# A decoder layer on one core: other buffers and another place for the first feed-forward weights and read-backs

## The chip, the core and the metric

The kernel runs on one core of a Trainium2 chip. A core has a matrix engine (TensorE, here PE, with its weight loads as PEld), three engines for element work (VectorE or DVE, ScalarE or ACT, GpSimd or POOL) and a queue engine (SyncE or SP) that here only issues transfers. Each works off its own queue in order; semaphores order them against each other. The metric is the device time of one execution in microseconds (us).

## What is computed

One layer of a decoder on 1024 tokens of width 1024, all in float32: a projection, four heads of a gated delta rule, four heads of differential attention, an output product with a residual, and a gated feed-forward part of width 2816. The change touches the end of attention, the output product and the feed-forward part:

```python
proj = rms_norm(h, norm1_w[l]) @ w_in[l]
...
mix = jnp.concatenate([o_a.reshape(B_, S_, DN_V), o_b.reshape(B_, S_, DF_V)], axis=-1)
h = h + mix @ w_out[l]
u = causal_dwconv(rms_norm(h, norm2_w[l]) @ w_up[l], ffn_conv_w[l], ffn_conv_b[l])
gate, up = jnp.split(u, 2, axis=-1)
h = h + (jax.nn.silu(gate) * up) @ w_down[l]
```

## The kernel before

**Products in three.** Each float32 matrix is split into a high part (a copy by ACT into a shorter form) and a low part (what is left, a subtraction by DVE or POOL); a product is then three matmuls, high by high, high by low and low by high. `split_w` (line 200) does it for weights, `mm3` (line 382) issues the three matmuls.

**Buffers.** Tiles are 128 partitions by 1024 columns and come from pools with a fixed number of buffers each: "g" has 16, "w" 5, "raw" 3 (loads from memory), "l" 2, "j" 2, "c" 4. A tile that wants a buffer waits until an earlier tile of the same pool has seen its last reader. A planner puts the instructions of each engine in an order ahead of time: by their place in the program, moved forward by the number that `part(name)` takes from the table `PRI` (line 36), and by when it thinks their inputs and buffers are there.

**From attention to the feed-forward part.** Attention runs head by head over eight row tiles of 128 tokens; in the last head the tiles run from 7 down to 0. `wout_a` (line 1030) multiplies the first half of the mixed heads with the output weights during heads 1 to 3 and keeps the result in memory. `wout_b` (line 1107) does the second half in the last head, one row tile at a time: load, product, residual, normalization, transposes (`norm_T`), and `combine` (line 1069). Its eight weight tiles (two column halves `c`, two row halves, high and low) take their buffers from the list `spare` in line 1111, and POOL makes their low parts (line 204).

**The up product by seven products.** The normalized activations are cut in token halves and width halves, the weights in gate and up and in width halves, and these two-by-two products are done with seven block products rather than eight. `combine` stores the blocks "11" and "21" for tiles 7 to 4, and for tiles 3 to 0 the block "22", the combination T2 (in its two parts) and the rests T1, T3 and T4, which `mv_split` (line 1211) splits afterwards. `product` (line 1222) is 12 matmuls of 128x512. `up_early` (line 1246) does the products "11" and "21" of the first two of 22 weight tiles ahead of the others, since they need only tiles 7 to 4; its load is held back until a named result of the last head (`o3`) exists, by a one-element copy on POOL into the load's buffer (line 1249). `up` (line 1260) loads a weight tile, forms four sums on POOL, splits them, and issues T2, "11", T1, T3, "21", "22" and T4; the result goes through the depthwise convolution, `silu` and the gate and is written to `act_dram`, 128 rows for each `j`. It uses four "c" buffers (cg, cu and two acc).

**The down product.** `down` (line 1318) runs over the two column halves, and in each over 11 pairs of 128 rows of the activations: it loads and splits the pair's weights, reads the two activation tiles back from `act_dram` (line 1336), splits them (lines 1338 and 1339) and issues 48 matmuls into eight PSUM banks, one for each row tile. The banks are in two pools of four; `bank(i, s)` takes one from pool `i % 2`, and the last up tile (j = 21) uses pool 1.

Of the kernel before, what the change touches and what calls it, by code (L numbers as in the profile page):

```python
# [34 lines left out]

PRI = dict(dprep=1000, dscan=930, dinv=200, dout=100, dproj=100, dz1=100, qk0=370, v0=400,
           d_dec=0, d_k=-25, d_q=0, d_nat=50, d_sc=800, d_v=0, d_w=-430, qkn=970, qks=25, a2o=0,
           prep0=160, attn1=0, attn2=0, attn3=25, prep=-25, fill=0, wa=0, wb1=0, wb2=25, ffn=110)
FS = [2, 1, 2, 3, 2, 2, 2, 2]
PP0, PP1 = 4, 2  # L40
PRE_K = {5: 1, 6: 0}
# [17 lines left out]
def hybrid_layer(ctx, tc, x, positions, norm1_w, w_in, dn_conv_w, dn_a_log, dn_dt_bias,  # L59
# [1009 lines left out]
    def combine(pss, u, tt):  # L1069

        o = slice(tt % 4 * P, tt % 4 * P + P)
        by = lambda ap: ap.rearrange("p (k t) -> p k t", t=P)
        if tt == NT - 1:
            mv_new("11")
            mv_new("21")
        if tt == 3:
            mv_new("22")
            mv_new("T2")
        if tt >= 4:
            if tt % 2 == 1:  # L1080
                stage[tt], stage[tt - 1] = ([gt("k1"), gt("k4")],) * 2
            half = slice(tt % 2 * 512, tt % 2 * 512 + 512)
            for q, name in enumerate(("11", "21")):
                hv, lv = (t[:, :, o] for t in stage[name])
                S.activation(hv, by(pss[q]), AF.Copy)
                V.tensor_tensor(lv, by(pss[q]), hv.bitcast(F32), op=ALU.subtract)
                S.activation(stage[tt][q][:, half], pss[q], AF.Copy)
            return
        b12, b22 = pss
        t1, t4 = (t[:, tt % 2 * 512:tt % 2 * 512 + 512] for t in stage[tt + 4])  # L1090
        t2 = u[:, 0:512]
        if tt % 2 == 1:
            stage["T3"] = stage.get("T3", []) + [gt("t3")]
        t3 = stage["T3"][-1][:, tt % 2 * 512:tt % 2 * 512 + 512]
        S.activation(t3, b12, AF.Copy)
        V.tensor_tensor(t1, b12, t1, op=ALU.subtract)
        V.tensor_tensor(t2, b22, t1, op=ALU.subtract)
        V.tensor_tensor(t3, b22, t3, op=ALU.subtract)
        hv, lv = (t[:, :, o] for t in stage["22"])
        S.activation(hv, by(b22), AF.Copy)  # L1100
        V.tensor_tensor(lv, by(b22), hv.bitcast(F32), op=ALU.subtract)  # L1101
        hv, lv = (t[:, :, o] for t in stage["T2"])
        S.activation(hv, by(t2), AF.Copy)
        G.tensor_tensor(lv, by(t2), hv.bitcast(F32), op=ALU.subtract)
        G.tensor_tensor(t4, t4, t2, op=ALU.subtract)

    def wout_b():

        w2row = gt("w2row")
        nc.scalar.dma_start(w2row, norm2_w.broadcast_to([P, D]))  # L1110
        spare = itertools.chain([wt] * 5, [ltr] * 2, [jtr])
        wfs = [load_wo(4, c, G, lambda s: next(spare)(s)) for c in range(2)]

        def tile_(tt):
# [90 lines left out]
    def bank(i, s):  # L1205
        return pf[i % 2].tile([P, 512], F32, tag="b", name=nm(s))
# [1 line left out]

    act_dram = dp.tile([FFN, T], F32, name="act_dram")

    def mv_split(name, src, lo_eng):

        tiles = [[gtr("x" + name) for _ in range(2)] for _ in range(2)]
        mv[name] = [[tiles[p][k // 2][:, k % 2 * 512:k % 2 * 512 + 512] for k in range(4)] for p in range(2)]
        for tt in (3, 2, 1, 0):
            sv = src(tt).rearrange("p (k t) -> p k t", t=P)
            for i in range(2):
                hv, lv = (tiles[p][i].rearrange("p (k t) -> p k t", t=512)[:, :, tt * P:tt * P + P] for p in range(2))
                S.activation(hv, sv[:, 2 * i:2 * i + 2], AF.Copy)
                lo_eng.tensor_tensor(lv, sv[:, 2 * i:2 * i + 2], hv.bitcast(F32), op=ALU.subtract)  # L1220

    def product(ps, w, name, start):

# [14 lines left out]
    def raw_(s="raw"):  # L1238
        return rp.tile([P, T], F32, tag="raw", name=nm(s))
# [5 lines left out]

    def up_early(j):

        e_raw = raw_()
        G.tensor_copy(e_raw[:, 0:1], o3[1][:, 0:1])
        load_half(e_raw, 0, j * P, 8)  # L1250
        w11, w12 = halves(split_w(e_raw, None, T, gtr))
        kept = gt("early")
        e = bank(1, "pe")
        product(e, w11, "11", True)
        S.activation(kept[:, 0:512], e, AF.Copy)  # L1255
        product(e, w12, "21", False)
        S.activation(kept[:, 512:1024], e, AF.Copy)
        return kept
# [59 lines left out]
    def down():  # L1318
        pairs = [(i, i + 1) for i in range(0, NF, 2)]
        kept = None  # L1320
        for c in range(2):
            cs = slice(c * 512, (c + 1) * 512)
            pss = [bank(1 - tt // 4, "pd") for tt in range(NT)]
            order = pairs if c == 0 else pairs[::-1]
            for pr in order:
                raw = raw_()
# [5 lines left out]
                else:  # L1332
                    hl = []
                    for i in pr:
                        g_ = ct_("act")
                        nc.sync.dma_start(g_, act_dram[i * P:(i + 1) * P, :])
                        gh, gl = gtr("gh"), gtr("gl")
                        S.activation(gh, g_, AF.Copy)  # L1338
# [22 lines left out]
                    V.tensor_tensor(rv[:, i, :], pss[tt], rv[:, i, :], op=ALU.add)  # L1361
                    nc.sync.dma_start(out2[tt * P:(tt + 1) * P, cs], rv[:, i, :])

    with part("ffn"):
        early = [up_early(j) for j in range(EARLY)]
    mv_split("T1", lambda tt: stage[tt + 4][0][:, tt % 2 * 512:tt % 2 * 512 + 512], V)
    mv_split("T3", lambda tt: stage["T3"][1 - tt // 2][:, tt % 2 * 512:tt % 2 * 512 + 512], V)
    mv_split("T4", lambda tt: stage[tt + 4][1][:, tt % 2 * 512:tt % 2 * 512 + 512], G)
    for j in range(NF):
        up(j, early[j] if j < EARLY else None)  # L1370
    down()
# [28 lines left out]
```

## Time and profile before

| | us |
|---|---|
| median of 3 runs | 1448.12 |
| lowest and highest | 1446.78 and 1448.77 |
| the profiled execution, its own time | 1446.19 |
| its span, first to last instruction | 1444.5 |
| PE busy | 1340.6 |
| DVE busy | 886.0 |
| ACT busy | 612.0 |
| POOL busy | 388.2 |

Busy time is the sum of the instructions' durations on an engine; a matmul's end is modelled, so a full PE is not PE at its peak. The granted clock is PE's, as a share of full speed. In a timeline, the brackets behind an instruction give the idle time of its engine before it and what ended that; where an engine waited for several things, it is the one that came last.

### The profile page before, as it was taken

Reading aid. Unit: us, or ns where it says so; the run is one execution under the profiler, and the core shown is the slowest. Engines: PE = TensorE matmul, PEld = TensorE weight load, DVE = VectorE, ACT = ScalarE, POOL = GpSimd, SP = SyncE. Lnnn points to the kernel's source line nnn. Section 1 sums busy time; section 2 is a strip of 40 time slices with the busy share of each in tenths; the row PEclk is TensorE's granted clock in tenths of the full one; section 3 lists DMA queues with packets and bytes.
Section 4 is the critical chain, followed back from the end, with each engine's and each line's share of the span. In section 5 each row is a group of like instructions: output and inputs, shape, how many; then the busy total and the mean of one; then the engine's idle time right before and its main releaser. Section 6 shows DMA issues by size and latency. Waiting matters only on the chain. (4 is left out here: it accounts for less than half of the span.)

```text
span 1444.5 us, 20625 instructions
## 1 busy us (share of the span) xinstructions
PE 1340.6 (93%) x7927; PEld 1128.8 (78%) x7927; DVE 886.0 (61%) x1745; ACT 612.0 (42%) x1098; POOL 388.2 (27%) x307
## 2 busy tenths in 40 slices
PE   7998898989979998998878999999999988999998
PEld 7877676888979986786656788888888876888887
DVE  5467978886343378886778666666666655324322
ACT  6445454532334456573545444343434434222220
POOL 3044313130341253321035434444433320000000
PEclk8999999999999999999998999999999998999999
DMA  7221112131743357443521222222222237447421
GB/s 222 84 79 36 39 30 74 43 91 59 194 107 94 117 154 187 113 126 102 175 81 44 88 82 79 88 88 78 82 88 85 76 120 276 144 160 215 150 88 59
DMA packets 143393, 155.14 MB, mean 107 GB/s; under 512 B 9279, under 2 KB 114367, under 8 KB 143295
## 3 DMA queue, kind: packets, MB, share of 16 engines
q1 hardware_dynamic: 130815, 144.14, 31.3%
q0 software_dynamic: 11008, 8.39, 3.1%
q10 hardware_dynamic: 1472, 1.29, 0.3%
q8 instruction: 62, 1.02, 0.3%
q14 instruction: 36, 0.29, 0.1%
HBM read 111.32 MB, written 38.29 MB: 104 GB/s over the span
## 5 line engine op out<-in xcount | busy, mean ns | idle before, releaser
L383 PE MATMUL pd<-whi,gh 128*128 128x512 f32 x352 | 138.3, 393 | 7.0 <-ACT gh L1338 7.0
L385 PE MATMUL pd<-whi,gl 128*128 128x512 f32 x352 | 138.1, 392 | 0.7 <-DVE gl L1339 0.7
L204 POOL TENSOR_TENSOR wlo<-raw,whi 128x1024 fp32r<-128x1024 f32 x34 | 83.6, 2468 | 203.9 <-PE gT L424 68.7
L384 PE MATMUL pd<-wlo,gh 128*128 128x512 f32 x352 | 138.1, 392 | 0.0
L1315 POOL TENSOR_TENSOR acc<-acc,acc 128x1024 f32<-128x1024 f32 x22 | 53.5, 2432 | 241.6 <-issue 196.6
L403 PE MATMUL pn<-whi,xn 128*128 128x256 f32 x448 | 114.8, 290 | 0.0
L404 PE MATMUL pn<-whi,xn 128*128 128x256 f32 x448 | 114.2, 289 | 0.0
L1338 ACT ACTIVATE gh<-act 128x1024 fp32r<-128x1024 f32 x42 | 44.4, 1060 | 134.6 <-PE pd L384 113.8
L1339 DVE TENSOR_TENSOR gl<-act,gh 128x1024 fp32r<-128x1024 f32 x42 | 51.8, 1237 | 67.8 <-ACT gh L1338 67.6
L403 PEld LDWEIGHTS pn<-whi,xn 128*128 128x128 f32 x448 | 85.9, 192 | 0.4
L404 PEld LDWEIGHTS pn<-whi,xn 128*128 128x128 f32 x448 | 85.9, 192 | 0.1
L383 PEld LDWEIGHTS pd<-whi,gh 128*128 128x128 f32 x352 | 66.8, 190 | 21.5 <-ACT gh L1338 7.5
L206 DVE TENSOR_TENSOR wlo<-rx,whi 128x1024 fp32r<-128x1024 f32 x22 | 29.5, 1339 | 87.5 <-ACT whi L202 87.5
L202 ACT ACTIVATE whi<-raw 128x1024 fp32r<-128x1024 f32 x58 | 61.0, 1052 | 50.8 <-issue 18.3
L1230 PE MATMUL pa<-xT,whi 128*128 128x512 f32 x176 | 71.2, 404 | 9.2 <-DVE x L1101 4.8
L424 PE MATMUL gT<-xn,wlo 128*128 128x512 f32 x192 | 78.7, 410 | 0.0
L385 PEld LDWEIGHTS pd<-whi,gl 128*128 128x128 f32 x352 | 66.7, 190 | 15.2 <-DVE gl L1339 1.4
L422 PE MATMUL gT<-xn,whi 128*128 128x512 f32 x192 | 78.2, 407 | 0.0
L206 DVE TENSOR_TENSOR wlo<-raw,whi 128x1024 fp32r<-128x1024 f32 x24 | 30.1, 1254 | 78.3 <-PE pd L384 57.9
L423 PE MATMUL gT<-xn,whi 128*128 128x512 f32 x192 | 77.7, 405 | 0.0
L384 PEld LDWEIGHTS pd<-wlo,gh 128*128 128x128 f32 x352 | 66.8, 190 | 14.0
L1230 PE MATMUL pe<-x,whi 128*128 128x512 f32 x176 | 70.6, 401 | 5.5 <-ACT early L1255 4.4
(378 smaller groups left out, 3744.8 us busy)
## 6 DMA issues: line engine op xcount, KB each, us to landing
act<-act_dram SPq DMA_DIRECT2D x42, 512.0 KB, 4.5
rw<-in_w_up_dram SPq DMA_DIRECT2D x22, 512.0 KB, 3.8
act_dram<-acc SPq DMA_DIRECT2D x22, 512.0 KB, 2.6
raw<-in_w_down_dram SPq DMA_DIRECT2D x22, 512.0 KB, 4.4
raw<-in_w_in_dram SPq DMA_DIRECT2D x18, 512.0 KB, 4.1
pn_dram<-pn SPq DMA_DIRECT2D x16, 512.0 KB, 4.2
rx<-in_w_up_dram SPq DMA_DIRECT2D x22, 256.0 KB, 2.9
rz<-in_w_up_dram SPq DMA_DIRECT2D x22, 256.0 KB, 3.3
```

The costliest lines, as they stand in the source:

```text
L202: S.activation(hi, raw[:, 0:w], AF.Copy)
L204: G.tensor_tensor(lo, raw[:, 0:w], hi.bitcast(F32), op=ALU.subtract)
L206: V.tensor_tensor(lo, raw[:, 0:w], hi.bitcast(F32), op=ALU.subtract)
L383: PE.matmul(ps, lh, rh, start=first, stop=False)
L384: PE.matmul(ps, lh, rl, start=False, stop=False)
L385: PE.matmul(ps, ll, rh, start=False, stop=last)
L403: PE.matmul(o, xs(xn, 0, kt, a, b), wh, start=kt == 0, stop=False)
L404: PE.matmul(o, xs(xn, 1, kt, a, b), wh, start=False, stop=False)
L422: PE.matmul(o, whi[:, kt, :], xs(x_, 0, kt, *qs), start=kt == 0, stop=False)
L423: PE.matmul(o, whi[:, kt, :], xs(x_, 1, kt, *qs), start=False, stop=False)
L424: PE.matmul(o, wlo[:, kt, :], xs(x_, 0, kt, *qs), start=False, stop=kt == NK - 1)
L1230: PE.matmul(ps, wh[:, ks], xh[k], start=first, stop=False, skip_group_check=not start)
```

## The change

Seven edits. (1) The first down pair's two read-back tiles take "raw" buffers in place of "c", and row tiles 0 to 3 of the down product take PSUM pool 0, the others pool 1, in place of the reverse. (2) The eight tiles of `wout_b`'s weights take, in order, two "l", one "j", one "w" and four "g" buffers, in place of five "w", two "l" and one "j". (3) The load and split of `up_early`'s weights move forward by 300 in place of 110, and the products and copies of `up_early` are no longer moved. (4) Its load is held back until result 5 of the last head, in place of result 1 (the tiles run from 7 down). (5) Its split weights take "w" buffers in place of "g". (6) `mv_split` goes two row tiles at a time, in half as many instructions twice as long, and the low parts of T4, which POOL made, are made by DVE. (7) The low part of T2 in `combine` is made by DVE in place of POOL.

```diff
--- before.py
+++ after.py
@@ -35,7 +35,7 @@
 
 PRI = dict(dprep=1000, dscan=930, dinv=200, dout=100, dproj=100, dz1=100, qk0=370, v0=400,
            d_dec=0, d_k=-25, d_q=0, d_nat=50, d_sc=800, d_v=0, d_w=-430, qkn=970, qks=25, a2o=0,
-           prep0=160, attn1=0, attn2=0, attn3=25, prep=-25, fill=0, wa=0, wb1=0, wb2=25, ffn=110)
+           prep0=160, early_w=300, early=0, attn1=0, attn2=0, attn3=25, prep=-25, fill=0, wa=0, wb1=0, wb2=25, ffn=110)
 FS = [2, 1, 2, 3, 2, 2, 2, 2]
 PP0, PP1 = 4, 2
 PRE_K = {5: 1, 6: 0}
@@ -1101,14 +1101,14 @@
         V.tensor_tensor(lv, by(b22), hv.bitcast(F32), op=ALU.subtract)
         hv, lv = (t[:, :, o] for t in stage["T2"])
         S.activation(hv, by(t2), AF.Copy)
-        G.tensor_tensor(lv, by(t2), hv.bitcast(F32), op=ALU.subtract)
+        V.tensor_tensor(lv, by(t2), hv.bitcast(F32), op=ALU.subtract)
         G.tensor_tensor(t4, t4, t2, op=ALU.subtract)
 
     def wout_b():
 
         w2row = gt("w2row")
         nc.scalar.dma_start(w2row, norm2_w.broadcast_to([P, D]))
-        spare = itertools.chain([wt] * 5, [ltr] * 2, [jtr])
+        spare = itertools.chain([ltr] * 2, [jtr], [wt], [gtr] * 4)
         wfs = [load_wo(4, c, G, lambda s: next(spare)(s)) for c in range(2)]
 
         def tile_(tt):
@@ -1208,16 +1208,16 @@
 
     act_dram = dp.tile([FFN, T], F32, name="act_dram")
 
-    def mv_split(name, src, lo_eng):
+    def mv_split(name, srcs):
 
         tiles = [[gtr("x" + name) for _ in range(2)] for _ in range(2)]
         mv[name] = [[tiles[p][k // 2][:, k % 2 * 512:k % 2 * 512 + 512] for k in range(4)] for p in range(2)]
-        for tt in (3, 2, 1, 0):
-            sv = src(tt).rearrange("p (k t) -> p k t", t=P)
+        for g in (1, 0):
+            sv = srcs[g].rearrange("p (b k t) -> p k b t", b=2, t=P)
             for i in range(2):
-                hv, lv = (tiles[p][i].rearrange("p (k t) -> p k t", t=512)[:, :, tt * P:tt * P + P] for p in range(2))
+                hv, lv = (tiles[p][i].rearrange("p (k g b t) -> p k g b t", k=2, g=2, t=P)[:, :, g] for p in range(2))
                 S.activation(hv, sv[:, 2 * i:2 * i + 2], AF.Copy)
-                lo_eng.tensor_tensor(lv, sv[:, 2 * i:2 * i + 2], hv.bitcast(F32), op=ALU.subtract)
+                V.tensor_tensor(lv, sv[:, 2 * i:2 * i + 2], hv.bitcast(F32), op=ALU.subtract)
 
     def product(ps, w, name, start):
 
@@ -1245,10 +1245,11 @@
 
     def up_early(j):
 
-        e_raw = raw_()
-        G.tensor_copy(e_raw[:, 0:1], o3[1][:, 0:1])
-        load_half(e_raw, 0, j * P, 8)
-        w11, w12 = halves(split_w(e_raw, None, T, gtr))
+        with part("early_w"):
+            e_raw = raw_()
+            G.tensor_copy(e_raw[:, 0:1], o3[5][:, 0:1])
+            load_half(e_raw, 0, j * P, 8)
+            w11, w12 = halves(split_w(e_raw))
         kept = gt("early")
         e = bank(1, "pe")
         product(e, w11, "11", True)
@@ -1320,7 +1321,7 @@
         kept = None
         for c in range(2):
             cs = slice(c * 512, (c + 1) * 512)
-            pss = [bank(1 - tt // 4, "pd") for tt in range(NT)]
+            pss = [bank(tt // 4, "pd") for tt in range(NT)]
             order = pairs if c == 0 else pairs[::-1]
             for pr in order:
                 raw = raw_()
@@ -1332,7 +1333,7 @@
                 else:
                     hl = []
                     for i in pr:
-                        g_ = ct_("act")
+                        g_ = raw_("act") if c == 0 and pr is order[0] else ct_("act")
                         nc.sync.dma_start(g_, act_dram[i * P:(i + 1) * P, :])
                         gh, gl = gtr("gh"), gtr("gl")
                         S.activation(gh, g_, AF.Copy)
@@ -1361,11 +1362,11 @@
                     V.tensor_tensor(rv[:, i, :], pss[tt], rv[:, i, :], op=ALU.add)
                     nc.sync.dma_start(out2[tt * P:(tt + 1) * P, cs], rv[:, i, :])
 
-    with part("ffn"):
+    with part("early"):
         early = [up_early(j) for j in range(EARLY)]
-    mv_split("T1", lambda tt: stage[tt + 4][0][:, tt % 2 * 512:tt % 2 * 512 + 512], V)
-    mv_split("T3", lambda tt: stage["T3"][1 - tt // 2][:, tt % 2 * 512:tt % 2 * 512 + 512], V)
-    mv_split("T4", lambda tt: stage[tt + 4][1][:, tt % 2 * 512:tt % 2 * 512 + 512], G)
+    mv_split("T1", [stage[5][0], stage[7][0]])
+    mv_split("T3", stage["T3"][::-1])
+    mv_split("T4", [stage[5][1], stage[7][1]])
     for j in range(NF):
         up(j, early[j] if j < EARLY else None)
     down()
```

## Rows read from the trace of the kernel before

**Rows 1.** First part of the page: busy time, share of the span and instructions.

```profile
PE 1340.6 (93%) x7927; PEld 1128.8 (78%) x7927; DVE 886.0 (61%) x1745; ACT 612.0 (42%) x1098; POOL 388.2 (27%) x307
```

**Rows 2.** Busy time by stretch, with clock and DMA (columns in the first line).

```profile
core 0: us, PE busy (x) PEld busy (x) DVE busy (x) ACT busy (x) POOL busy (x), PEclk, DMA share, GB/s
615.00:645.00 30.00, 29.76 (x203) 25.50 (x204) 23.29 (x57) 22.76 (x55) 3.33 (x5) 1.00 0.42 126
645.00:660.00 15.00, 9.69 (x58) 7.89 (x56) 13.24 (x20) 6.20 (x15) 10.00 (x4) 0.94 0.31 101
660.00:670.00 10.00, 9.60 (x50) 8.54 (x50) 7.09 (x30) 5.02 (x18) 0.00 (x0) 0.75 0.23 75
728.40:769.00 40.60, 24.83 (x96) 18.33 (x97) 33.61 (x59) 21.41 (x42) 21.76 (x17) 0.85 0.22 72
769.00:775.00 6.00, 5.99 (x16) 4.77 (x17) 5.18 (x12) 3.17 (x11) 2.88 (x4) 0.57 0.01 1
1170.00:1189.90 19.90, 17.40 (x70) 13.70 (x68) 11.00 (x13) 6.65 (x7) 3.23 (x1) 0.91 0.42 133
1197.00:1204.20 7.20, 6.53 (x15) 4.65 (x16) 3.25 (x3) 2.11 (x2) 0.75 (x1) 0.50 0.90 328
1204.20:1400.00 195.80, 195.80 (x865) 162.12 (x864) 74.52 (x66) 58.38 (x57) 0.00 (x0) 1.00 0.52 167
```

**Rows 3.** Timeline, 1150 to 1200 us: SP's queue, DVE and PE.

```profile
1162.05 7.91 SPq L1327 DMA_DIRECT2D raw<-in_w_down_dram  x3
...
1175.58 1.22 DVE L206 TENSOR_TENSOR wlo<-raw,whi 128x1024 fp32r<-128x1024 f32 x1
...
1192.53 3.05 SPq L1336 DMA_DIRECT2D act<-act_dram  x2
...
1197.02 0.80 PE L383 MATMUL pd<-whi,gh 128*128 128x512 f32 x1 [7.05 <-ACT gh L1338]
```

**Rows 4.** Timeline, 660 to 780 us: DVE, POOL and ACT.

```profile
668.74 0.35 DVE L944 SCALAR_TENSOR_TENSOR s<-s,rs,subw 128x128 f32<-128x128 f32 x1
...
706.46 0.30 POOL L1249 COPY raw<-s 128x1 f32<-128x1 f32 x2 [51.32 <-DVE rst L197]
...
720.87 1.21 ACT L1087 ACTIVATE k<-tr 128x512 f32<-128x512 f32 x2
...
740.51 1.05 ACT L202 ACTIVATE whi<-raw 128x1024 fp32r<-128x1024 f32 x1
```

**Rows 5.** Timeline of PE, 726 to 772 us: start, duration, what; wait and releaser.

```profile
730.12 0.50 PE L383 MATMUL pwo<-whi,mhl 128*128 128x512 f32 x1 [1.76 <-ACT mhl L1054]
...
741.61 0.50 PE L1230 MATMUL pe<-x,whi 128*128 128x512 f32 x1 [1.08 <-ACT whi L202]
...
754.05 1.04 PE L246 MATMUL tr<-k_sb,u 128*128 128x128 f32 x8
...
758.82 0.80 PE L1230 MATMUL pe<-x,whi 128*128 128x512 f32 x1 [3.74 <-ACT early L1255]
...
769.01 0.77 PE L1230 MATMUL pa<-xT,whi 128*128 128x512 f32 x1 [4.80 <-DVE x L1101]
```

**Rows 6.** Timeline, 640 to 661 us: POOL, DVE and PE.

```profile
645.13 10.00 POOL L204 TENSOR_TENSOR wlo<-raw,whi 128x1024 fp32r<-128x1024 f32 x4 [26.31 <-PE pwo L384]
...
645.41 2.17 DVE L917 SCALAR_TENSOR_TENSOR sums<-sums,nlam 128x1 f32<-128x1 f32 x1
...
659.71 0.58 PE L903 MATMUL S<-K,Q 128*128 128x256 f32 x1 [3.51 <-ACT p L913]
```

**Rows 7.** Groups by line, 722 to 775; last row: line 1220 alone, ns min/median/max.

```profile
L1096 DVE TENSOR_TENSOR k<-tr,k 128x512 f32<-128x512 f32 x4 | 2.8, 688 | 1.3 <-ACT t L1095 1.3
L276 DVE SCALAR_TENSOR_TENSOR u<-hrow,rs,w2row 128x1024 f32<-128x1024 f32 x4 | 5.1, 1282 | 0.1
L197 DVE SCALAR_TENSOR_TENSOR rst<-rs,rsh 128x1 f32<-128x1 f32 x9 | 2.7, 306 | 0.2
...
L1220 DVE TENSOR_TENSOR xT<-k,xT x8: 407/1306/1542, 760.2 to 769.5; 128x256 fp32r<-128x256 f32 x8
```

## The prediction

> **What bounds the kernel now.** I read the page's first part, then busy time by stretch, then the timeline of each stretch in which TensorE (PE) was not full. PE is busy for 93% of the span, DVE for 61% [rows 1], so the bound is PE almost everywhere, and an edit pays only where PE stands still or runs at its lower clock. The table by stretch shows where [rows 2]: 615 to 645 us and 1204.2 to 1400 us are full at clock 1.00 (865 matmuls in 195.8 us, 0.226 us each), and three places are not. One: 645 to 660, 9.69 of 15 us busy, and 660 to 670 at clock 0.75. Two: 728.4 to 769, 24.83 of 40.6 busy at clock 0.85, and behind it 769 to 775 at 0.57. Three: a wait of 7.05 us up to 1197.02 [rows 3], and behind it 1197 to 1204.2 at 0.50, the lower of the two levels (1.2 of 2.4 GHz). The last is the cleanest to read, so I begin there. The rest of the kernel I leave as it is: the edits touch nothing before the fourth head's weights are asked for, and nothing in the steady loop over 22 up tiles.
>
> **Up to down (lines 1323 and 1335).** The last up tile's last product ends near 1189.9. The first down matmul starts at 1197.02 and is released by the split of the first activation tile, whose read-back is issued at 1192.53 [rows 3]. That moment is not when the data are there (rows 0 and 1 were written twenty tiles earlier): the read-back goes into one of the four "c" buffers, and cg, cu and two acc of the last up tile hold all four until its convolutions end. Beside it the weights of the first pair were split at 1175.58, and their three loads had gone out from 1162.05 on [rows 3]. The edit takes the first pair's two tiles from the three "raw" buffers instead, which come free in the 1160s as those loads show. Two read-backs then take the places of the second and third weight load, which come later by the time of one split.
> With that the data are no longer late; next would be the banks. In the kernel before, row tiles 0 to 3 of the down product sit in the pool that the last (odd) up tile uses; the edit swaps the pools, so the first 12 matmuls write banks that the tile before has left, and the others begin 12 x 0.226 = 2.7 us later, about 1192.6: by then the last up result has been added out, since the convolution that reads it stands right behind the issue of 1192.53. The split work (two ACT copies of 1.05 us, two DVE subtractions of 1.22 us, by the same shape [rows 3, 4]) moves from the gap into the last up tile. ACT is busy for 6.65 and DVE for 11.0 of its last 19.9 us, so it fits; but PE too is busy for only 17.4 of these [rows 2], since the subtraction of 1.22 us at 1175.58 stands in DVE's queue before an add that PE waits for [rows 3].
> Sum: the stall 7.05 us, a second one of 0.67 us after it, and the slow clock: 15 matmuls in 6.53 us, 0.435 each against 0.226, 15 x 0.209 = 3.1 us [rows 2, 3]. Together 10.8 us at most. One more such subtraction in PE's way takes off 1.2 us or a little more with the clock. I take 9.5; bounds 2 (only the swap of banks and a shorter load) and 10.8.
>
> **Into the up tiles (lines 36 to 38, 1104, 1111, 1211 to 1257).** In 728.4 to 769 PE stands idle for 15.8 us in eight waits, the three largest at 730.12, where the last output product starts, 758.82 and 769.01 [rows 5]. The slow clock adds: 12 matmuls from 758.82 at twice 0.226, 2.7 us, and 6 x 0.43 = 2.6 us after 769. In all some 21 us are there to win. What the waits say: the 48 early matmuls (48 x 0.226 = 10.9 us) could run once the first four normalized tiles are stored, at 722.1 [rows 4], but begin at 741.61, released by their weights' split. Those weights are requested at 706.46, behind the seventh result of head 4, and split only at 740.51 [rows 4]. Then they stand in PE's queue ahead of the last tile's transposes at 754.05, and ACT works off weight splits before that tile's evictions; so the first up product waits until 769.01 for the last tile's DVE work [rows 5].
> The edits: the request hangs on the third result instead (668.74, [rows 4]), 38 us sooner; the split goes into "w" buffers, of which four come free behind the first output product, on whose end POOL waits to 645.13 [rows 6], at priority 300; the early matmuls have no priority left, so the last tile's chain goes first and they fill its gaps. POOL's one-element copy now waits sooner; POOL has been idle for 51.32 us before it [rows 4] and has nothing due behind it but the combination of the last four tiles, which needs later data: free. The two loads go ahead of row loads on SP's queue, at the 0.37 us or so that an issue takes: under 1 us. Two ACT copies and two DVE subtractions (4.5 us in all) move some 60 us forward, into a stretch where PE has other tiles' work to cover them.
> How early can the first up product start? PE has 24 output matmuls, 24 transposes and 48 early matmuls left at 728.4, about 19.5 us: 748. DVE is later: before that product it must do 21 operations of 0.69 us (adds, combinations, and four subtractions for T2 that come over from POOL, line 1104), three of 1.28 us, some 27 short ones (0.31 us in line 197's row, which holds waits beside POOL; I use 0.2, so 5 us) and one weight split of 1.22 us, 24.5 us from 728.3: 752.8 [rows 7]. Against 769.0 that is 16.2 us, and with a warm clock 18.8. The merged activation splits: DVE goes from 16 of 0.41 us (the shortest, free of POOL) to 12 of 0.69 us, +1.7 us; ACT does 12 operations in place of 24, and POOL loses 8. These are needed one product (2.7 us) after another, and DVE remains the fuller engine, so I expect some 4 us to be given back there, and 3 us because a fixed order never fills every gap. I take 12; bounds 3 (only the early matmuls' own waits go) and 19.
>
> **The output weights (line 1111).** Four POOL subtractions in a row, 645.13 to 655.1, wait for "w" buffers. Beside them a DVE operation on 128x1 takes 2.17 us, and PE waits for what is delayed, 3.51 us at the longest [rows 6]. The place costs 15 - 9.69 = 5.3 us of standing still and 10 x 0.25 = 2.5 us of slow clock [rows 2], 8 us. Now the first half goes into "l" and "j" buffers and one free "w", so it can be split from about 617 on; the second half takes four "g" buffers. The POOL time stays, but is spread over 615 to 645, where PE is full yet DVE busy for 23.29 of 30 us [rows 2]: part of the delay will show there. Gain between -4 and +7; I take 2.
> Here a page speaks against the change. The rows show DVE held beside POOL: of eight subtractions the shortest took 0.41 us and the median, beside POOL's work, 1.31 us [rows 7]. The Trainium skill, page "SBUF — State Buffer", section "Who interferes with whom", says that a DVE instruction with two SBUF inputs waits for a GpSimd instruction that reads SBUF until it ends, and the trace agrees. By that rule each of the eight subtractions that come over from POOL can itself be held; that result is the first rival below.
>
> **Sum.** 9.5 + 12 + 2 = 23.5 us off the profiled execution's 1446.19 us (span 1444.5 and 1.7 around it) is 1422.7; the median of the runs, 1448.12, lies 1.9 us higher, so 1424.6, told as 1424.5.
>
> **Rivals.** (1) DVE becomes the bound into the up tiles. What speaks for this rival: it is busy for 33.61 of 40.6 us there and gets 2 x 4 x 0.69 = 5.5 us more; if each of these eight is held 0.9 us as the median in [rows 7], 7 more. Against it: at least half of the eight there are held already, some 4 us, which fewer POOL operations reduce. Then 12 becomes 2 to 3: 1434. (2) The down start is not won: the read-backs go out early but the next pair's, still in "c", is late, since those buffers come free at 1192.5 and later as now. Pair one covers 48 x 0.226 = 10.9 us, to 1201, and issue to use took 4.5 us [rows 3], so I doubt it. Gain 2 in place of 9.5: 1432. (3) Slower: the "g" buffers run short. Sixteen exist; until about 649 the old output weights hold 4, the attention pairs 6, the norm row 1 and now 4 more: 15. If two more are wanted before 649, the fourth head runs with one pair less in flight and each of seven tiles waits like the one at 659.71, 3.51 us and its slow clock, 1 to 2 us: 7 x 5 = 35 against 23.5, 1459. Two that would tip it (the normalized row and its pair of stage tiles) come after 680, which speaks against it. (4) The order around both places comes out as now, with no change: 1448.
>
> **Chances.** Forecast 0.60 (its own range 1417 to 1431), (1) 0.20, (2) 0.10, (3) 0.06, (4) 0.04. The range 1413 to 1440 takes in the forecast, its best bounds and the first two rivals, and leaves out (3) and (4). A change under 0.2%, about 3 us, can't be told from none. Faster 0.90, same 0.04, slower 0.06.
>
> **What would show it.** Right: no PE wait over 1 us between the last up and the first down matmul, and clock 1.00 there; the early weights' split before 700; the first T2 product about 25 us after the last output product's start rather than 39; POOL's four splits not in one block. Wrong: a wait on DVE of several us at that product (rival 1), a read-back as releaser of the second pair (rival 2), PE waits of 3 us at each tile of head 4 (rival 3).

## The result and the profile after

The changed kernel takes 1430.74 us (median of 4 runs, 1428.42 to 1434.71) against 1447.45 us for the kernel before beside it (4 runs, 1445.11 to 1448.77): a ratio of 0.9889, 95% interval 0.9863 to 0.9915, or 16.7 us between the medians. Run a second time, beside the last three experiments, it stood at 0.986 (0.9828 to 0.9892). The forecast was 23.5 us. The profiled execution took 1430.1 us, its span is 1428.4.

First the page's first part, which answers to [rows 1]. PE has 6.1 us less work in the modelled sum, DVE 7.7 and POOL 11.2; the shares of the span stay within one point.

```profile
PE 1334.5 (93%) x7927; PEld 1126.6 (79%) x7927; DVE 878.3 (61%) x1745; ACT 611.3 (43%) x1086; POOL 377.0 (26%) x295
```

Busy time by stretch, for the places of [rows 2] (columns in the first line). The last two rows are the 20 us before the end of the last up product and the 14.2 us behind it.

```profile
core 0: us, PE busy (x) PEld busy (x) DVE busy (x) ACT busy (x) POOL busy (x), PEclk, DMA share, GB/s
615.00:645.00 30.00, 27.61 (x174) 22.73 (x173) 20.56 (x43) 20.87 (x46) 12.96 (x11) 1.00 0.44 119
645.00:660.00 15.00, 14.78 (x103) 12.90 (x102) 11.85 (x39) 8.24 (x24) 0.00 (x0) 1.00 0.27 94
660.00:670.00 10.00, 9.98 (x61) 8.43 (x60) 8.08 (x31) 4.67 (x16) 0.30 (x2) 1.00 0.42 125
...
740.00:753.40 13.40, 7.95 (x28) 5.98 (x29) 12.44 (x23) 7.29 (x13) 4.54 (x4) 0.82 0.14 42
753.40:760.60 7.20, 1.94 (x8) 1.57 (x8) 3.85 (x5) 3.73 (x7) 4.78 (x4) 0.50 0.00 0
760.60:775.00 14.40, 13.55 (x50) 10.71 (x51) 10.75 (x15) 4.25 (x8) 0.45 (x1) 0.83 0.07 20
1165.20:1185.20 20.00, 15.56 (x60) 12.10 (x60) 12.24 (x14) 7.88 (x9) 3.24 (x1) 0.91 0.55 170
1185.20:1199.40 14.20, 14.20 (x64) 11.75 (x64) 9.44 (x9) 6.56 (x6) 2.40 (x1) 1.00 0.73 248
```

Two of the three thin places are gone: 645 to 660 is full at clock 1.00 (POOL has nothing there, where [rows 6] had four splits), and the start of the down product holds 64 matmuls at full clock. The third, between the last output product and the up products, is still there. In the last up tile PE now stands still longer than in [rows 2]: 15.56 of 20 us against 17.40 of 19.9.

PE's timeline shows the waits that are left (start, duration, what; in brackets the wait and its releaser). The row of 760.65 answers to the last of [rows 5], that of 1185.02 to the last of [rows 3]. Line numbers are those of the kernel that was run, so some move by a few between kernels. `whi` and `wlo` are the two parts of weights, `x` and `xT` those of the up product's activations, `gh` and `gl` those of the read-back tiles; `pa`, `pc` and `pe` are the banks of an up tile, `pd` those of the down product, and `cg` and `cu` collect the gate and up rows.

```profile
740.47 0.63 PE L246 MATMUL tr<-k_sb,u 128*128 128x128 f32 x4 [4.09 <-DVE x L1101]
...
753.43 1.94 PE L246 MATMUL tr<-k_sb,u 128*128 128x128 f32 x8 [4.58 <-DVE u L276]
760.65 0.80 PE L1230 MATMUL pa<-xT,whi 128*128 128x512 f32 x1 [5.28 <-ACT xT L1103]
...
1170.13 0.50 PE L1230 MATMUL pe<-x,whi 128*128 128x512 f32 x1 [2.46 <-ACT cu L1289]
...
1173.76 0.50 PE L1230 MATMUL pa<-xT,whi 128*128 128x512 f32 x1 [1.98 <-DVE cg L1281]
...
1185.02 0.39 PE L383 MATMUL pd<-whi,gh 128*128 128x512 f32 x1
```

**Where the time went.** Two executions drift apart before the first changed instruction. So I count from a common point, a POOL addition on line 871 (515.80 us in the kernel before, 517.77 in the changed one), ahead of which the kernels are alike, to four moments: the start of the first T2 product; the start of the last product (T4) of the sixth up tile, where the loop runs steadily in all kernels; the end of the last up product; the end of the span. The last two columns are worked out: what lies between the sixth tile and the end, and the change against the kernel before at the sixth tile.

| kernel | T2 | sixth tile | last up ends | end | sixth tile to end | at sixth tile |
|---|---|---|---|---|---|---|
| before | 253.2 | 361.6 | 674.2 | 928.7 | 567.1 | |
| changed | 242.9 | 352.0 | 667.4 | 910.6 | 558.6 | -9.6 |
| changed, again | 243.6 | 352.7 | 668.2 | 911.4 | 558.7 | -8.9 |
| w1, output weights only | 250.1 | 358.5 | 671.1 | 925.7 | 567.2 | -3.1 |
| w3, w1 and early weights | 236.0 | 350.5 | 663.2 | 918.0 | 567.5 | -11.1 |
| u1, all but the down edits | 243.4 | 352.3 | 663.5 | 918.2 | 565.9 | -9.3 |
| d1, down edits only | 255.9 | 364.2 | 679.0 | 922.2 | 558.0 | +2.6 |
| d2, its read-back half | 256.0 | 364.4 | 679.2 | 922.4 | 558.0 | +2.8 |
| d3, its bank half | 253.1 | 361.6 | 674.1 | 928.6 | 567.0 | 0.0 |
| x1, changed, `gl` on POOL | 243.5 | 352.6 | 670.7 | 913.9 | 561.3 | -9.0 |
| h1, changed, weights held | 238.1 | 352.7 | 665.8 | 908.9 | 556.2 | -8.9 |
| p1, changed, T2 on POOL | 241.8 | 352.0 | 664.9 | 908.1 | 556.1 | -9.6 |
| z1, h1 and p1 | 240.6 | 349.7 | 665.1 | 908.3 | 558.6 | -11.9 |
| z3, z1, another gate | 242.7 | 353.5 | 668.6 | 911.8 | 558.3 | -8.1 |

Read the sixth column first. It falls into two groups: 565.9 to 567.5 without the new read-back, 556.1 to 558.7 with it, and 561.3 in x1 between them. The seventh is less sharp: d1, d2 and the kernel before issue the same instructions in the same order up to the last up tiles, and d1 and d2 are still 2.6 and 2.8 us behind it at the sixth tile. The granted clock goes with it, in the 15 us from the last row tile's `mhl` split (line 1055), first of the kernel before, then of d2:

```profile
730.90:745.90 15.00, 10.21 (x45) 7.73 (x46) 14.50 (x35) 5.91 (x12) 6.05 (x5) 0.92 0.27 91
```

```profile
731.70:746.70 15.00, 10.72 (x42) 7.78 (x42) 13.03 (x31) 5.97 (x12) 5.58 (x5) 0.78 0.22 77
```

From the start of the last output product to the first T2 product it is 40.8 us in d1 and d2 (clock 0.77 and 0.78), 38.9 in the kernel before and in d3 (0.92). So a difference under 3 us in the seventh column says nothing alone. The sum for the changed kernel is -9.6 and -8.5, 18.1 us; 2.0 are lost ahead of the common point in this execution, which leaves the 16.1 of the spans.

### The profile page after: what moved, and what is told of

Its sections match the earlier page's. It is cut to its first block, busy times and chain, and to the rows that moved or that the text cites. A ratio compares the mean times of both kernels' runs of the same rounds, so it can differ in the third digit from the quotient of the medians.

```text
span 1428.4 us, 20608 instructions
## 1 busy us (share of the span) xinstructions
PE 1334.5 (93%) x7927; PEld 1126.6 (79%) x7927; DVE 878.3 (61%) x1745; ACT 611.3 (43%) x1086; POOL 377.0 (26%) x295
## 3 DMA queue, kind: packets, MB, share of 16 engines
q10 hardware_dynamic: 1472, 1.29, 0.3%
## 5 line engine op out<-in xcount | busy, mean ns | idle before, releaser
L202 ACT ACTIVATE whi<-rx 128x1024 fp32r<-128x1024 f32 x22 | 23.3, 1061 | 127.4 <-POOL rx L1271 127.4
## 6 DMA issues: line engine op xcount, KB each, us to landing
rx<-in_w_up_dram SPq DMA_DIRECT2D x22, 256.0 KB, 2.8
rz<-in_w_up_dram SPq DMA_DIRECT2D x22, 256.0 KB, 3.3
```

Source lines behind the costliest of these rows:

```text
L202: S.activation(hi, raw[:, 0:w], AF.Copy)
```

## The experiments

**The down edits (d1), all the others (u1), the output weights (w1).**

```diff
# d1: on the kernel before
-            pss = [bank(1 - tt // 4, "pd") for tt in range(NT)]
+            pss = [bank(tt // 4, "pd") for tt in range(NT)]
...
-                        g_ = ct_("act")
+                        g_ = raw_("act") if c == 0 and pr is order[0] else ct_("act")
# u1: the changed kernel with these two lines as before
# w1: on the kernel before
-        spare = itertools.chain([wt] * 5, [ltr] * 2, [jtr])
+        spare = itertools.chain([ltr] * 2, [jtr], [wt], [gtr] * 4)
```

> The kernel before with only the two edits of the down product: the first pair's read-backs in raw buffers and the banks of row tiles 0 to 3 in pool 0. Theory (the gain there is the removed stall and slow clock, less what the moved splits cost inside the last up tile): no PE wait at the first down matmul in place of 7.05 us, a new PE wait of about 2.5 us in the last up tile, 8 to 9 us faster in all, 0.994 of before. Rival (the splits moved into the last up tile cost nothing by themselves, and the loss of 3.6 us seen there in the changed kernel comes from the other edits): 10 to 11 us faster, no new wait.

> The changed kernel with the two down edits undone. Theory (the stages add): 7 to 8 us faster than before, 0.995, with the stall of 7 us back at the first down matmul. Rival (the two ends of the up stretch share one gain, because DVE or the clock gives it back in between): under 4 us faster.

> The kernel before with only the other buffers for the second half's output weights; the early up weights stay in g buffers, so both want g at once. Theory (the four POOL subtractions leave the block of 645 to 655 and DVE is no longer held there): the PE waits of 1.8 and 3.51 us between 645 and 660 go, the first tile's transposed row is split 5 to 6 us earlier counted from 517 us, and what is won stays up to the first up product: 4 to 6 us faster, 0.997. Rival (g buffers run short in the fourth head): PE waits of 3 us at its tiles, 1.005 or more. Rival (the 5 to 6 us come from the early weights or from drift between executions): 1.000.

Measured: d1 0.993 (0.9909 to 0.9952), u1 0.9936 (0.9911 to 0.9961), w1 0.9969 (0.995 to 0.9988). The ratios of d1 and u1 multiply to 0.9866, within the interval of the whole: two independent parts of nearly the same size. For d1 one new wait of about 2.5 us was on record; the trace has two in the last up tile, 2.15 and 1.06 us, in place of the one of 2.50 us of the kernel before, and 9.1 us less from the sixth tile to the end. In u1 the wait of 7.05 us is back, as forecast. The place where they differ is plain in u1, in the 14.2 us behind its last up product; the changed kernel has 64 matmuls there (above), u1 has 15, as before:

```profile
1180.20:1194.40 14.20, 6.52 (x15) 4.64 (x16) 8.12 (x8) 5.47 (x5) 2.35 (x1) 0.66 0.74 245
```

w1 lost the waits of 1.80 and 3.51 us in the fourth head, and tile 7's transposed rows came 5.2 us sooner (144.9 after the common point against 150.1); 3.1 of these were left at the sixth tile, in an execution with the lower clock shown above for d2 (0.78). At the tiles behind, PE waits for 2.31 us at the longest (2.30 before), and the one new wait, 1.45 us for a transfer at 634.18, is a single one, so the rival of "g" buffers that run short, with 3 us at each tile, is out.

**The two halves of the down edit (d2, d3).** d2 is the kernel before with the second line of d1's diff alone, d3 with the first.

> The kernel before with one half of the down edit: the first pair's activations are read into the raw buffers, the banks of the down products stay in the old order. Theory (both halves are needed): the first down product no longer waits for the ACT split (7.05 us before), but its bank is the one that the last up tile's DVE additions still read, so it waits for DVE's last addition, some 1.5 to 3.5 us, and the splits that now stand in the last up tile add a wait of about 2 us there as they did with the whole down edit: 2 to 4 us less than before, ratio 0.997 to 0.9985. Rival (the bank order is idle): no wait of over 0.5 us at the first down product and the whole gain of the down edit, ratio 0.993.

> The kernel before with the other half: the banks of the down products in the new order, the activations still read into the ct buffers. Theory: the wait of about 7 us on the ACT split stays at the first down product, since the buffers come free no sooner, and the time is within 0.1% of before. Rival: if the bank were the later of the two, the wait would shrink by 2 us or more and the ratio be 0.998 or below.

Measured: d2 0.9921 (0.9907 to 0.9934), the whole gain; d3 0.9991 (0.9977 to 1.0004), none, with its wait of 7.05 us for the split (`gh`) unchanged. In d2 the first down product follows the last up product at once, in the old order of banks. PE's timeline of d2:

```profile
1179.89 0.50 PE L1230 MATMUL pe<-x,whi 128*128 128x512 f32 x1 [2.16 <-ACT cu L1288]
...
1183.52 0.79 PE L1230 MATMUL pa<-xT,whi 128*128 128x512 f32 x1 [1.01 <-DVE cg L1280]
...
1194.64 0.39 PE L1232 MATMUL pa<-xT,w 128*128 128x512 f32 x1
1194.87 0.39 PE L383 MATMUL pd<-whi,gh 128*128 128x512 f32 x1
```

The theory on record (both halves are needed) fell; its rival holds. By the code an up tile takes three banks (pa, pc, pe) of a pool of four, so one is free at any rate; PE waits for none of the others either. The first two rows are the price: with the splits moved into the last up tile PE is held twice there (once for 2.50 us in the kernel before). The planner's order differs as well: six matmuls of product "21" now stand ahead of T3, between the two waits, where all twelve came behind it.

**The low parts of the first pair on POOL (x1).**

```diff
-                        V.tensor_tensor(gl, g_, gh.bitcast(F32), op=ALU.subtract)
+                        (G if c == 0 and pr is order[0] else V).tensor_tensor(gl, g_, gh.bitcast(F32), op=ALU.subtract)
```

> The changed kernel with the two low-part subtractions of the first down pair on POOL in place of DVE. In the changed kernel PE waits 2.46 us for ACT's copy of a product and 1.98 us for DVE's addition in the last up tile, and two such subtractions of 1.23 us each stand on DVE there (1161.89 and 1169.55), while POOL is idle for 18 us. Theory (the moved splits cost this): without them DVE runs 1.2 us earlier ahead of both waits, their sum falls from 4.4 us to 2 to 3 us, and the kernel is 1.5 to 2.5 us shorter, ratio to before 0.987. Rival (POOL's subtraction reads SBUF beside DVE and holds DVE's instructions with two SBUF inputs for its own 2.5 to 3 us): the additions and convolution steps of DVE around 1162 to 1173 lengthen, the waits stay at 4.4 us or grow to 7, and the kernel is the same or up to 3 us longer.

Measured: 0.9899 (0.9885 to 0.9914), and 561.3 us from the sixth tile to the end against 558.6. The rival holds: one wait of 7.19 us (up to 1177.22, for DVE's addition `cg`) in place of 2.46 and 1.98. Not all of it is DVE's: in x1 the six matmuls of "21" that stand between the two waits of the changed kernel are behind T3 again. From the end of product T1 to T3 it is 7.19 us against 6.09, 1.1 us more; most of the rest of the 2.7 us is that order. DVE's and POOL's timeline of x1:

```profile
1164.77 2.59 DVE L206 TENSOR_TENSOR wlo<-rz,whi 128x1024 fp32r<-128x1024 f32 x1 [4.96 <-ACT whi L202]
...
1170.87 4.56 DVE L1311 SCALAR_TENSOR_TENSOR acc<-cu,fcw,acc 128x1023 f32<-128x1023 f32 x2
```

```profile
1163.87 2.40 POOL L1340 TENSOR_TENSOR gl<-act,gh 128x1024 fp32r<-128x1024 f32 x1 [7.89 <-ACT gh L1339]
1171.46 2.89 POOL L1340 TENSOR_TENSOR gl<-act,gh 128x1024 fp32r<-128x1024 f32 x1 [5.19 <-ACT gh L1339]
```

In the changed kernel the same DVE instructions take 1.22 us, and 1.28 and 1.29. The first one here starts 0.90 us after POOL's, which ends at 1166.27, and ends 1.09 behind that, at 1167.36: it did nearly nothing beside POOL. What DVE was spared, 2 x 1.23 us, came back as 1.37 and 1.99, 0.9 us more than was spared. The Trainium skill, page "SBUF — State Buffer", section "Who interferes with whom", says that a DVE instruction with two SBUF inputs contends with a GpSimd instruction that reads SBUF, by an exclusive lock on a shared port pair; these rows agree.

**The weights of the first up tiles held (h1), T2's low part back on POOL (p1).** The traces above named two suspects for the late T2 product: ACT's queue, where weight splits that wait for POOL stand ahead of the last row tile, and DVE's load. ACT's and DVE's timeline of the changed kernel:

```profile
736.06 1.06 ACT L202 ACTIVATE whi<-rx 128x1024 fp32r<-128x1024 f32 x1 [3.78 <-POOL rx L1271]
...
739.84 1.06 ACT L273 ACTIVATE u<-hrow 128x1024 f32<-128x1024 f32 x1
...
756.12 1.06 ACT L202 ACTIVATE whi<-rx 128x1024 fp32r<-128x1024 f32 x1 [6.12 <-POOL rx L1271]
757.08 0.61 ACT L1219 ACTIVATE xT<-k 128x512 fp32r<-128x512 f32 x1
757.60 0.58 ACT L1095 ACTIVATE t<-tr 128x512 f32<-128x512 f32 x1
```

```profile
750.91 2.37 DVE L276 SCALAR_TENSOR_TENSOR u<-hrow,rs,w2row 128x1024 f32<-128x1024 f32 x1
753.39 1.57 DVE L1220 TENSOR_TENSOR xT<-t,xT 128x512 fp32r<-128x512 f32 x1
758.21 0.69 DVE L1096 TENSOR_TENSOR k<-tr,k 128x512 f32<-128x512 f32 x1 [3.25 <-ACT t L1095]
```

```diff
# h1: on the changed kernel, in up(); sq0 is the last row tile's sum of squares
+        if j < EARLY:
+            G.tensor_copy(y_[:, 0:1], sq0[0])
         load_half(w_, 0, upc, 8)
# p1: on the changed kernel, in combine(), T2
-        V.tensor_tensor(lv, by(t2), hv.bitcast(F32), op=ALU.subtract)
+        G.tensor_tensor(lv, by(t2), hv.bitcast(F32), op=ALU.subtract)
```

> The changed kernel with one more dependency: the POOL sums of the first two up weight tiles wait, through a copy of one element, until the last row tile's sum of squares exists, so their splits can't stand ahead of that square in ACT's queue. Theory (the first up product is late because ACT waits 3.78 us for POOL with the last tile's chain behind it): the square starts 3 us or more earlier, counted from that tile's split row, the first up product starts 31 us after that row in place of 34.9, and the time falls by 2 to 4 us. Rival (DVE is full there and sets the start): the square is earlier and the first up product is not; time as the changed kernel. Rival (the sums themselves are then late): the first up product waits for its weights, 1 to 3 us slower.

> The changed kernel with the low part of the T2 activations back on POOL (one line undone). It tests the forecast's rival that DVE's load sets the start of the up products. If DVE set it: two of its instructions of 0.68 us between tile 0's transposes and the first T2 product go, and that product comes 0.7 us or more sooner. Theory (ACT's queue sets it, and DVE was idle for 3.25 us there): POOL's instruction of 1.28 to 1.46 us stands behind its own additions for up(1) and takes the place of 0.68 us on DVE, so the product comes 0.5 to 2 us later and the kernel is 0 to 2 us longer, ratio to before 0.989 to 0.991.

Measured: h1 0.9857 (0.9834 to 0.988), p1 0.9847 (0.9831 to 0.9863); both overlap the changed kernel's 0.986 (0.9828 to 0.9892), and p1 only touches the first interval. The new dependency moved other instructions too: h1's order differs from the changed kernel's from about 660 us on, and its last output product starts 4.0 us later (211.8 after the common point against 207.8). Its T2 product comes 26.3 us behind that in place of 35.1, so 4.8 us sooner, and nothing of it is left at the sixth tile (352.7 against 352.0), since new waits follow. PE's timeline of h1:

```profile
756.06 0.76 PE L1232 MATMUL pa<-xT,whi 128*128 128x512 f32 x1 [2.97 <-ACT xT L1103]
758.97 0.79 PE L1233 MATMUL pa<-xT,whi 128*128 128x512 f32 x1 [2.15 <-DVE xT L1104]
...
766.62 0.80 PE L1234 MATMUL pc<-xT,wlo 128*128 128x512 f32 x1 [1.52 <-DVE wlo L206]
```

p1's T2 product comes 1.1 us sooner, where the theory on record had it 0.5 to 2 later (two executions of the changed kernel differ by 0.7 us there), and the sixth tile is where it was. So in these traces neither alone moves the loop. At the end h1 and p1 are still 1.7 and 2.5 us ahead of the changed kernel. That arises in the last up tiles, which their edits don't touch: from the sixth tile to the end of the last up product they take 313.1 and 312.9 us against 315.4, and the clock over the last 20 us is 1.00 in both, 0.91 in the changed kernel.

**Both together (z1), with another gate (z3), and the changed kernel beside them (a1).** z1 is h1 and p1; z3 holds the second tile's weights until the last row tile's T3 block exists.

> The changed kernel, unaltered, beside the three others of this group, so that they are compared on one chip. It should stand at a ratio of 0.987 to 0.9895 to the kernel before and 9 to 10 us of the forecast's 23.5 short of nothing: 15 to 19 us are won.

> The changed kernel with the weights of the first two up tiles held until tile 0's sum of squares is there, and with the low part of the T2 activations back on POOL. Each alone shortened the profiled execution, by 1.7 and 2.5 us from a common point before the change's first edit. Theory (ACT's order and DVE's load are two separate terms of the shortfall into the up products): the gains add, some 4 us below the changed kernel, ratio to it 0.997. Rival (both open the same stretch, and the up weights' splits then set the products): no more than the better of the two, 2.5 us, and a wait of over 2 us for the weights' low parts within the first up tile.

> As the run before it, but the second up tile's weights are held until tile 0's T3 activations exist, later than its sum of squares. Theory (ACT's split of the second tile's weights, which waited 6.12 us for POOL ahead of tile 0's copies, costs the first T2 product): that product comes 1 to 4 us sooner than with the first gate, and the kernel is 1 to 3 us shorter than that. Rival (the weights of the second up tile are then late): a wait of 2 us or more at the second up tile's first product takes it back, and the times agree within 0.1%.

Measured, on one chip: a1 0.986 (0.9828 to 0.9892; 1425.62 to 1434.33 us), z1 0.9825 (0.9797 to 0.9853; 1422.63 to 1429.42), z3 0.9828 (0.98 to 0.9857). a1 won 19.9 us between the medians, a little more than the 15 to 19 on record. z1 has the lowest median of all kernels here, 1425.61 us against 1432.23 for the changed one. The intervals against the kernel before overlap, but the six runs of each can be compared directly: on average z1 lies 5.7 us below a1 (95% interval about 2 to 9.5, worked out from these runs), z3 5.2 us. So the gain on record, some 4 us, is borne out by the times. Its reason isn't: the 1.7 and 2.5 us that it adds up arose in the last up tiles (above). In the one trace of each, z1's sixth tile comes 2.3 us sooner than the changed kernel's, by the table no more than one execution's own variation. z3's T2 product came later than z1's, not sooner, and its time is the same: the second gate gives nothing.

**The early weights without the new splits (w3).** The kernel before with w1's line and the new `up_early` (edits 3 to 5), but `mv_split`, T2 and the down product as before.

> The kernel before with the output weights' buffers and the early up weights' edits, without the new order of the activations' splits, without T2's low part on DVE and without the down edits. Output weights alone gave 0.9969, all but the down edits 0.9936. Theory (most of the gain into the up products is the early weights', split in gaps instead of beside tile 0's chain, so that the early products fill PE's waits): the first T2 product comes 244 to 247 us after the common point against 250 with the output weights alone, ratio 0.994 to 0.9955. Rival (the splits of the activations are what was won): that product stays within 1 us of 250 and the ratio at 0.997.

Measured: 0.9904 (0.9873 to 0.9934), beyond what either side expected. The T2 product starts at 236.0, 7.4 us before that of u1, which differs from it only in the order and engine of the activations' splits (edits 6 and 7). Its absolute time is 752.09 us. But PE's and DVE's timeline of w3 show it waiting again at once:

```profile
752.09 0.50 PE L1230 MATMUL pa<-xT,whi 128*128 128x512 f32 x1 [3.01 <-ACT xT L1103]
753.89 0.80 PE L1231 MATMUL pa<-xT,whi 128*128 128x512 f32 x1 [1.30 <-POOL xT L1104]
757.97 0.79 PE L1232 MATMUL pa<-xT,wlo 128*128 128x512 f32 x1 [3.29 <-DVE wlo L206]
```

```profile
756.17 1.74 DVE L206 TENSOR_TENSOR wlo<-rx,whi 128x1024 fp32r<-128x1024 f32 x1
757.84 1.74 DVE L206 TENSOR_TENSOR wlo<-ry,whi 128x1024 fp32r<-128x1024 f32 x1
```

By stretch, w3 up to that product and behind it: DVE is busy for 12.86 of 13.00 us and for 7.48 of 7.90.

```profile
739.10:752.10 13.00, 8.86 (x37) 6.77 (x37) 12.86 (x30) 10.30 (x27) 5.09 (x5) 0.87 0.08 23
752.10:760.00 7.90, 3.31 (x7) 2.10 (x8) 7.48 (x8) 3.92 (x10) 7.54 (x7) 0.61 0.08 25
```

The weights' low parts stood in DVE's queue behind the activations'. 6.1 of the 17.2 us of the start are given back by the sixth tile, and there w3 is only 1.8 us ahead of u1 (350.5 and 352.3), which is within the variation. On the same chip w3 is 5.7 us above a1 on average (interval about 1 to 10), less than the 8.5 us of the read-back that it lacks. Edits 6 and 7 thus gave nothing that these runs can tell; if anything they cost.

## Why the prediction was right, and where it was off

**The time.** 1430.74 us lies within the range of 1413 to 1440, but at the edge of the forecast's own range (1417 to 1431), and nearer to rivals 2 (1432) and 1 (1434) than to 1424.5. The time alone doesn't tell these apart; the traces do.

**What bounds it.** Right: all that was won was won in the three thin places, and the loop between is as long as before (567.1 us from the sixth tile to the end in the kernel before, 567.5 in w3).

**Up to down, 9.5 forecast, 8.5 measured.** Three of the four terms held. The wait of 7.05 us, the second one and the slow clock were summed to 10.8: behind the last up product, 14.2 us hold 15 matmuls in u1 and 64 in the changed kernel, 49 x 0.226 = 11.1 us. The fourth, 1.2 us for one more subtraction in PE's way, was too small. The last up product ends 3.9 us later after the common point than in u1, 667.4 against 663.5, but part of that is the clock, which stayed at 1.00 over the last 20 us of u1's up tiles:

```profile
1160.20:1180.20 20.00, 17.33 (x76) 13.70 (x74) 12.45 (x14) 7.95 (x9) 3.24 (x1) 1.00 0.41 132
```

In the changed kernel, the kernel before and w3 it is 0.91. Against the last two the price is 2.7 to 2.8 us from the sixth tile to the end of the last up product (315.4 against 312.6 and 312.7), with two waits in the last tile where there was one. DVE's and ACT's timeline of the changed kernel show where it comes from:

```profile
1161.89 1.23 DVE L1340 TENSOR_TENSOR gl<-act,gh 128x1024 fp32r<-128x1024 f32 x1 [5.45 <-ACT gh L1339]
...
1169.55 1.23 DVE L1340 TENSOR_TENSOR gl<-act,gh 128x1024 fp32r<-128x1024 f32 x1
...
1173.01 0.69 DVE L1281 TENSOR_TENSOR cg<-pa,cu 128x512 f32<-128x512 f32 x1
```

```profile
1168.54 1.06 ACT L1314 ACTIVATE acc<-acc 128x1024 f32<-128x1024 f32 x1 [0.85 <-DVE acc L1311]
1169.50 0.58 ACT L1289 ACTIVATE cu<-pe 128x512 f32<-128x512 f32 x1
```

From 1161.89 to the addition `cg` at 1173.01 DVE has no idle time, and both moved subtractions stand in that run, not one. The other wait, for ACT's copy that empties pe, goes back to DVE too: the copy stands behind an instruction that waited 0.85 us for DVE's convolution step. The step on the banks was wrong: nothing waited for them, and of the lower bound of 2 the swap's share is 0 (d3). The second rival, a late second pair, is out: no wait stands there.

**Into the up tiles, 12 forecast, about 4 to 6.5 measured.** Here the sum failed. With the output weights the forecast was 14; the sixth tile came 9.6 us sooner (8.9 in a1), of which the output weights have 3.1 to 5.2. The step that failed is "DVE is later: 752.8", by which the first T2 product comes about 25 us behind the start of the last output product rather than 39. That start in the changed kernel, and the busy time from there to the T2 product, first of the changed kernel, then of h1:

```profile
725.58 0.50 PE L383 MATMUL pwo<-whi,mhl 128*128 128x512 f32 x1
```

```profile
725.60:760.60 35.00, 20.66 (x89) 16.06 (x88) 27.25 (x55) 16.86 (x29) 16.07 (x12) 0.83 0.22 72
729.80:756.10 26.30, 18.40 (x90) 14.07 (x89) 25.83 (x52) 15.03 (x26) 11.89 (x11) 1.00 0.35 106
```

With the T2 product at 760.65 it is 35.1 us in the changed kernel, against 38.9 in the kernel before. The count of DVE's operations was fair: in h1, where DVE is busy for 25.83 us, it is 26.3. But the step took DVE as an engine that never waits. In the changed kernel it is busy for only 27.25 of 35.0 us. Of the rest, 3.25 us are ahead of the last tile's first combination, because ACT's split for the second up tile waited 6.12 us for POOL ahead of the copy that this needs, and 3.07 us end at 738.49, released by a split of the first up tile's weights behind ACT's wait of 3.78 us for POOL. That w3 starts at 752.09, close to the 752.8 forecast, is chance: its last output product starts at 724.10, 6 us sooner than in the kernel before, and the T2 product 28.0 us behind it. The second half of the step, that an earlier start is worth its distance less some 4 us (and 3 for gaps), held roughly in w3 (6.1 of 17.2 us given back) and not in h1, where 4.8 us more of start were worth nothing. A reading that fits, but which no run tests by itself: what counts is when DVE is through with the whole first tile's low parts, activations and weights, not when its first product starts; the sum priced one weight split of these and only up to that start. Rival 1 named the engine that is full in w3 and h1, and was wrong in its price for the changed kernel: of the four T2 subtractions moved to DVE only one was held (1.26 us, the others 0.68), not each by 0.9.

**The output weights, 2 forecast.** Right in sign, small: 5.2 us at tile 7, 3.1 at the sixth up tile, 4.5 by the ratio of w1 (0.0031 x 1448). The delay that was feared in 615 to 645 is there, PE 27.61 of 30 us against 29.76 in [rows 2] (with a new wait of 1.33 us for a transfer at 628.29), and 645 to 670 gives back more.

**What was forecast to be seen.** No wait before the first down matmul and clock 1.00: yes. The early weights' split before 700: yes, at 672.21 and 677.85. POOL's four splits apart: yes, none in 645 to 660. The first T2 product about 25 us after the last output product's start: no, 35.1. A wait on DVE of several us at the T2 product, the sign for rival 1: in part, 5.28 us, but released by ACT. The signs for rivals 2 and 3: no.

**What stays open.** Edits 3 to 5 were run only together, and 6 and 7 only by the difference of w3 and u1 (7 also in p1). Why the sixth tile comes no sooner than about 350 us after the common point in any of these kernels isn't settled. In w3 DVE is full from 739.1 to 760; in the changed kernel no engine is, and their order differs in several places at once. w3's edits with the new read-back, which by these figures (an estimate) would lie near z1, were not tried.

## What to carry to other kernels

When a start is moved forward, price the moment at which the last input of that whole stage is ready, not the first; in h1 an earlier first product was worth nothing, since waits for the engine that makes the rest followed. Work taken out of a gap goes into the queues of the stage before it, so look on every engine for what stands behind it there, not only on the busiest. And split a two-part edit: here one line held the whole gain and its companion none.

## What was not expected of the hardware

DVE and POOL hold each other in both directions. In the changed kernel DVE's multiplication at 750.91 took 2.37 us beside a POOL addition of 1.26; in p1 DVE came first (754.08, 1.27 us) and POOL's addition, from 754.23, took 2.25. And the granted clock differs between executions of the same instructions: 0.92 and 0.78 in the same 15 us of the kernel before and of d2. d2 was 2.8 us behind at the sixth up tile, some 2 of them lost between the last output product and the T2 product, as much as several of the edits are worth. Over the last 20 us of the up tiles it was 0.91 in the changed kernel and 0.83 in z1, with the same order of products there.
